# Block 2's mixer: v and u before q and k, q and k with stationary weights, and three quarters of wo's pooled half ahead of the last heads' value products

## The chip, the cores and the metric

The kernel runs on one core of a Trainium2 chip. The metric is the device time of one execution in microseconds (us); lower is better. A core has a matrix engine (TensorE, PE in the profile; its weight loads are PEld), a vector engine (DVE), an activation engine (ACT), a small general engine (POOL), and a queue engine that issues DMAs (SP). Each engine works through its own list of instructions in the order in which the program holds them.

## The reference, cut to what matters

The program computes three transformer layers for 256 tokens of width 1024: twice a "first block", then one "second block" (block 2). The change lies in the mixer of block 2. In float32:

```python
h = rmsnorm(x, g_mix_pre) * (1 + scale_m) + shift_m       # 256 x 1024
q, k, v, u = split(h @ w_in)                              # each 256 x 512
z = q . k / sqrt(64)              # 8 heads of 64, keys before the query only
log1m = -softplus(z)              # masked
after = reverse_cumsum(log1m) - log1m
w = exp(log_sigmoid(z) + after)   # masked: stick-breaking weights
attn = w @ v                                              # 256 x 512
pool = ((trailing means of u over 2, 4, 8, 16 tokens) - u) @ w_pool * pool_scale
mix = concat(attn, pool) @ w_out                          # 256 x 1024
x = x + gate_m * rmsnorm(mix, g_mix_post)
```

A feed-forward part follows it and ends the program.

## The kernel before, in words

**Weights.** All weights come from one packed array in the order that `stream_order` lists. Each entry of the list is a chunk of two halves of 512 KB. SP loads a half into a `raw` tile (7 buffers). ACT then rounds it into a tile `H` (line 278) and DVE makes the remainder `L` = raw - H (line 280), 12 buffers each. A product of float32 exactness is made of three products of the rounded kind: H times the high part of the activations, H times their low part, and L times the high part. The activations are held in `Pair` tiles: `xm` for the normalised input of the mixer, `m` for its output (`m20` to `m23`: `m20` and `m21` hold the attention half, `m22` and `m23` the pooled half).

**Two forms of product.** `mmA4` keeps the activations stationary: for one of the two token tiles (t = 0 or 1, 128 tokens each), 24 matmuls of 512 columns give 128 tokens x 512 outputs. `mmB` keeps the weights stationary: for 128 outputs, 8 matmuls of 512 columns (both tiles' high and low parts side by side) and 8 of 256 columns give 128 outputs x 256 tokens, which is the transposed result. `mmD2` is a step of wo: two contraction chunks, one tile t, one half c of the output columns, 6 matmuls of 512 columns.

**Order on TensorE.** The program text is recorded in one order, and small pieces of work are put between the large products by a clock kept by hand: `pe(ns)` advances it, a generator that yields d is resumed by `tick()` once d us of this clock have passed. A scheduler then settles the order on each engine; `tc.high_priority` pulls instructions ahead, `issue_after` pins an order.

**The mixer of block 2.** `mixer2` makes q and k with `mmA4`, tile by tile; `turn` copies each result out (ACT, line 1005), lets TensorE transpose it (4 transposes into `pt2q` or `pt2k`, line 1009), and DVE copies it into `qT` or `kT` (line 1012). Then come v and u (`pv`, `pu`). Between these products stand the heads: `stick` handles four heads at a time, heads (0,1) of the pairs 0 and 1 as `z00` to `z11`, those of the pairs 2 and 3 as `z20` to `z31`. For each it makes the scores `z<-qT,kT`, then on DVE the mask and on ACT Abs, Exp and Ln and on DVE a sum (together softplus, into a tile `e1`), then on TensorE the running sums `z<-e1,tri`, on ACT an Exp, and then for the four heads together the value products `po2<-e1,v2`, whose result ACT and DVE put into `m` (lines 211, 212). `pool` makes, for each of the four groups g, `pl` (two matmuls with `pmat`), copies it out on ACT (`pm`, line 1040), multiplies by `w_pool` (`ppl`) and writes `m22` or `m23` on ACT and DVE (lines 1046, 1047).

**After the mixer.** The main text issues, on ACT's queue, five loads of gains and of modulation rows (`gpm`, `mpm`, `ggf`, `mgf`, `sh_f`), two of which DVE multiplies (`gpm`, `ggf`). Then the steps of wo follow. `WO2_LEAD` says how many of the four pairs (tile t, pooled chunk i) are recorded before the last heads are drained; the rest follows, with the norm of each tile (`Post`, `Norm`), and the feed-forward part begins with `pgA`.

Of the kernel before, what the change touches and what calls it, by code (L numbers as in the profile page):

```python
# [12 lines left out]
AF = mybir.ActivationFunctionType  # L13
ALU = mybir.AluOpType
# [30 lines left out]
TR_GAP = 0.0  # L45
LEAD = 1
MIX_DELAY = 2.5
WO2_LEAD = 2
UNIT = 10.0
SM_DELAY = 8.0  # L50
SOFT = 30
ST_DELAY = 8.0
ST_STEP = 3.5


# [38 lines left out]
def stream_order():  # L94
    o = []
    cond = list(COND)
    for l in range(DEPTH):
        o += [("q", l, c, h) for c in range(2) for h in range(2)]
        o += [("kv", l, h) for h in range(2)]
        for j in range(4):  # L100
            o += [("cc", l, j), ("cx", l, j), ("cb", l, j)]
        for n in ("cp", "gb", "ga", "ap"):
            o += four(n, l, take_cond(cond, n, l))
        o += [("wo", l, j) for j in range(4)]
        o += ffn_order(l, take_cond(cond, "ffn", l))
    assert not cond
    o += [("q2", h) for h in range(2)]
    o += [("k2", h) for h in range(2)]
    o += [("v2", h) for h in range(2)]
    o += [("u2", h) for h in range(2)]  # L110
    o += [("wo", 2, j) for j in (2, 3, 0, 1)]
    o += ffn_order(2, [])
    return o
# [5 lines left out]
def pack_weights(inp):  # L119
    splits = dict(q=0, kv=1024, cb=1536, cc=2560, cx=3584, ga=4608, gb=5632)  # L120
    out = np.empty((len(ORDER), P, CH), np.float32)

    def put(i, w, r0, nk, c0, nc_):
        src = w[r0:r0 + nk * P, c0:c0 + nc_]
        if nk == 4:
            out[i].reshape(P, nk, nc_)[...] = src.reshape(nk, P, nc_).transpose(1, 0, 2)
        else:
            out[i].reshape(P, 2, nk, nc_ // 2)[...] = src.reshape(nk, P, 2, nc_ // 2).transpose(1, 2, 0, 3)

    for i, k in enumerate(ORDER):  # L130
        n = k[0]
        if n == "q":
            put(i, inp["w_in"][k[1]], 512 * k[3], 4, 512 * k[2], 512)
        elif n == "kv":
            put(i, inp["w_in"][k[1]], 512 * k[2], 4, 1024, 512)
        elif n in ("cc", "cx", "cb"):
            put(i, inp["w_in"][k[1]], 0, 8, splits[n] + 256 * k[2], 256)
        elif n in ("ga", "gb", "cp", "ap"):
            w = {"cp": "w_conv_proj", "ap": "w_attn_proj"}.get(n, "w_in")
            put(i, inp[w][k[1]], 512 * (k[2] % 2), 4, splits.get(n, 0) + 512 * (k[2] // 2), 512)  # L140
        elif n == "cond":
            w = inp["w_cond_2"][0][:, 1024 * k[1]:1024 * (k[1] + 1)].reshape(D, P, KT)
            out[i].reshape(P, 2, D)[...] = w[:, :, 2 * k[2]:2 * k[2] + 2].transpose(1, 2, 0)
        elif n in ("q2", "k2", "v2", "u2"):
            put(i, inp["w_in_2"][0], 512 * k[1], 4, 512 * ("q2", "k2", "v2", "u2").index(n), 512)
        else:
            l = k[1]
            sfx, li = ("", l) if l < 2 else ("_2", 0)
            if n == "wo":
                put(i, inp["w_out" + sfx][li], 256 * k[2], 2, 0, 1024)  # L150
            elif n == "d":
                put(i, inp["w_down" + sfx][li], 256 * k[2], 2, 0, 1024)
            elif n in ("gA", "uA"):
                w = inp[("w_gate" if n == "gA" else "w_up") + sfx][li]
                put(i, w, 512 * k[2], 4, 0, 512)
            else:
                w = inp[("w_gate" if n == "g" else "w_up") + sfx][li]
                put(i, w, 0, 8, 512 + 256 * k[2], 256)
    return out
# [3 lines left out]
def tile_model(ctx: ExitStack, tc: tile.TileContext, x_in, wpack, sink, convw, gains, c_in,  # L163
# [55 lines left out]
    def spawn(gen, delay=0.0):  # L219
        tasks.append([clock[0] + delay, gen])  # L220

    def pe(ns):
        clock[0] += ns / 1000.0
# [20 lines left out]
            pass  # L244

    def mm(o, a, b, start, stop, **kw):
        nc.tensor.matmul(o, a, b, start=start, stop=stop, **kw)  # L247


    state = dict(raw=0, spl=0, use=0, behind=None, a=None, v=None)  # L250
# [699 lines left out]
    def stick(hps, qT, kT, v2, mp):  # L950

        rs = [slice(e * HD, (e + 1) * HD) for e in range(2)]
        hes = [(hp, e) for hp in hps for e in range(2)]
        z = {he: ps1(f"z{he[0]}{he[1]}") for he in hes}
        for hp in hps:
            for e in range(2):
                mm(z[hp, e][:, 0:T], kT[rs[e], hp, 0:P], qT[rs[e], hp, :], True, False, skip_group_check=True)
            for e in range(2):
                mm(z[hp, e][:, T:T + P], kT[rs[e], hp, P:T], qT[rs[e], hp, P:T], False, False, skip_group_check=True)
            pe(650)  # L960
        sps = {}
        for he in hes:
            zz = z[he][:, 0:384]
            z3 = zz.rearrange("p (b t) -> p b t", b=3)
            nc.vector.tensor_add(z3[:, 0:3:2, :], z3[:, 0:3:2, :], smask.unsqueeze(1).to_broadcast([P, 2, P]))
            e1 = s2(f"e1_{he[0]}{he[1]}", (P, 384))
            nc.scalar.activation(e1, zz, AF.Abs)
            nc.scalar.activation(e1, e1, AF.Exp, scale=-1.0)
            nc.scalar.activation(e1, e1, AF.Ln, bias=1.0)
            nc.vector.scalar_tensor_tensor(e1, zz, 0.0, e1, ALU.max, ALU.add)  # L970
# [21 lines left out]
    def mixer2(xp, norms):  # L992
        mp = Pair("m2")
        qT = s4("qT2", (P, 4, T))
        kT = s4("kT2", (P, 4, T))
# [1 line left out]
        u2t = s4("u2", (P, 2, 512))  # L997
        v2 = [v2t[:, t, :] for t in range(2)]
        cap = 2 * state["use"] + 8
        ww = {n: [get((n, h), cap) for h in range(2)] for n in ("q2", "k2")}  # L1000

        def turn(nm, t, ps, dstT, scl):
            tk = s2(f"tk2{nm}{t}")
            with ahead():
                state["behind"] = (nc.scalar.activation(tk, ps, AF.Copy, scale=scl), state["behind"][1])
            yield 1.5
            pt = ps1(f"pt2{nm}{t}", (P, 4, P))
            for k in range(4):
                nc.tensor.transpose(pt[:, k, :], tk[:, k * P:(k + 1) * P], ident)
                pe(107)  # L1010
            with ahead():
                nc.vector.tensor_copy(dstT[:, :, t * P:(t + 1) * P], pt)
            yield None

        for t in range(2):
            finish(norms[t].gen)
            for nm, dstT, scl in (("q2", qT, 0.125), ("k2", kT, 1.0)):
                ps = ps1(f"p2{nm}{t}")
                mmA4(ps, ww[nm], xp, t)
                spawn(turn(nm, t, ps, dstT, scl))  # L1020
                tick()
                if t == 0 and nm == "k2":
                    wv = [get(("v2", h), cap + 4) for h in range(2)]
        for i in range(2):
            spawn(stick((2 * i, 2 * i + 1), qT, kT, v2, mp), 3.0 + 4 * ST_STEP * i)
        for n, dst in (("v2", v2t), ("u2", u2t)):
            w = wv if n == "v2" else [get((n, h), cap + 8) for h in range(2)]
            for t in range(2):
# [24 lines left out]
        for g in range(4):  # L1053
            if g < 3:
                next(gens[g + 1])
            next(gens[g])
        return mp


# [166 lines left out]
```

## Time and profile before

| | |
|---|---|
| median of 3 runs | 1144.59 us (1143.29 to 1145.06) |
| the profiled execution | 1144.54 us, of which its span from first to last instruction is 1142.4 us |
| TensorE matmuls busy | 1132.2 us, 99% of the span |
| TensorE weight loads busy | 951.7 us, 83% |
| DVE busy | 800.3 us, 70% |
| ACT busy | 687.2 us, 60% |
| mean granted clock of TensorE | 0.998 of full speed |

The 2.1 us between the span and the time of the execution lie outside the recorded instructions. Busy times of TensorE are modelled from the starts of pipelined matmuls, so the distance from one start to the next is the better measure of what a matmul costs, and the rows below are read in that way.

### The profile page before, as it was taken

What the parts mean: (1) busy time and instruction counts of PE and PEld (TensorE: products, weight loads), DVE (VectorE), ACT (ScalarE), POOL (GpSimd) and SP (SyncE); (2) the same over time, 40 slices, a digit from 0 to 9 for tenths busy, and PEclk for the clock granted to TensorE, in tenths of its full rate; (3) what the DMA queues carried; (4) which work ended last, traced back from release to release, by engine and by line L of the source; (5) the groups of instructions that cost most, each with busy time, mean ns of one, the idle gap of its engine ahead of it and who ended that gap; (6) DMA issues with size and microseconds to landing.
All of it is one profiled execution on the core that took longest, in us unless ns stands there. A gap on an engine that the chain in (4) does not pass through costs nothing.

```text
span 1142.4 us, 15967 instructions
## 1 busy us (share of the span) xinstructions
PE 1132.2 (99%) x5901; PEld 951.7 (83%) x5901; DVE 800.3 (70%) x1188; ACT 687.2 (60%) x1209; POOL 13.4 (1%) x28
## 2 busy tenths in 40 slices
PE   8999999999999999999999999999999999999997
PEld 5888878888888888888878888888888778888886
DVE  7888745658977657798874758977657748866652
ACT  6778766547555446688765556545445847655441
POOL 0000000000000000000000000000000000000000
PEclk9999999999999999999999999999999999999999
DMA  7944346537987752835686538987773653855610
GB/s 286 367 131 160 118 148 210 187 137 253 351 286 244 248 203 85 303 129 166 203 269 211 178 118 275 354 275 243 254 265 104 228 167 110 312 185 185 200 58 37
DMA packets 67039, 235.39 MB, mean 206 GB/s; under 512 B 8849, under 2 KB 9361, under 8 KB 66962
## 3 DMA queue, kind: packets, MB, share of 16 engines
q1 hardware_dynamic: 63216, 224.83, 57.3%
q10 hardware_dynamic: 3746, 9.56, 2.5%
q8 instruction: 46, 0.75, 0.3%
q14 instruction: 31, 0.25, 0.1%
HBM read 233.28 MB, written 1.07 MB: 205 GB/s over the span
## 4 chain that ended last, share of the span: by engine, by line
PE 95%; DMA 2%; DVE 1%; issue 1%; ACT 0%; DVEq 0%; POOLq 0%; POOL 0%; ACTq 0%; SPq 0%
PE dn L247 15%; PE pu L247 14%; PE pg L247 13%; PE wo L247 5%; PE pcc L247 4%; PE pap L247 4%; PE pgb L247 4%; PE pga L247 4%; PE pcx L247 4%; PE pcp L247 4%; PE pcb L247 3%; PE pq L247 3%; PE puA L247 3%; PE pgA L247 3%; PE pkv L247 2%; PE po L247 1%
## 5 line engine op out<-in xcount | busy, mean ns | idle before, releaser
L280 DVE TENSOR_TENSOR L<-raw,H 128x1024 fp32r<-128x1024 f32 x370 | 445.4, 1220 | 141.1 <-ACT H L278 131.5
L278 ACT CAST H<-raw 128x1024 fp32r<-128x1024 f32 x370 | 383.5, 1052 | 153.8 <-issue 40.8
L247 PE MATMUL dn<-H,fHL 128*128 128x512 f32 x432 | 116.1, 390 | 0.0
L247 PE MATMUL pu<-xf,H 128*128 128x512 f32 x432 | 108.2, 392 | 0.0
L247 PE MATMUL pg<-xf,H 128*128 128x512 f32 x432 | 107.8, 391 | 0.0
L247 PEld LDWEIGHTS dn<-H,fHL 128*128 128x128 f32 x432 | 79.8, 188 | 15.6
L247 PEld LDWEIGHTS pg<-xf,H 128*128 128x128 f32 x432 | 79.2, 188 | 15.2
L247 PEld LDWEIGHTS pu<-xf,H 128*128 128x128 f32 x432 | 77.7, 189 | 13.9
L528 DVE SCALAR_TENSOR_TENSOR raw<-raw,silu_c 128x1024 f32<-128x1024 f32 x48 | 58.4, 1219 | 27.0 <-DMA raw<-in_wpack_dram 26.9
L247 PE MATMUL dn<-L,fHL 128*128 128x512 f32 x216 | 66.6, 389 | 0.0
L247 PEld LDWEIGHTS pg<-xf,L 128*128 128x128 f32 x432 | 58.9, 190 | 4.2
L247 PEld LDWEIGHTS pu<-xf,L 128*128 128x128 f32 x432 | 58.9, 190 | 4.2
L247 PE MATMUL pu<-xf,L 128*128 128x256 f32 x432 | 60.2, 282 | 0.0
L247 PE MATMUL pg<-xf,L 128*128 128x256 f32 x432 | 60.2, 282 | 0.0
L247 PE MATMUL wo<-H,m 128*128 128x512 f32 x192 | 52.9, 396 | 0.1
L575 ACT CAST fHL<-f 128x512 fp32r<-128x512 f32 x27 | 16.7, 620 | 54.1 <-DVE f L573 54.1
L247 PEld LDWEIGHTS dn<-L,fHL 128*128 128x128 f32 x216 | 40.5, 188 | 8.6
L569 ACT ACTIVATE s<-s 128x512 f32<-128x512 f32 x27 | 17.1, 632 | 43.4 <-DVE s L458 43.3
L247 PEld LDWEIGHTS wo<-H,m 128*128 128x128 f32 x192 | 35.4, 188 | 8.1 <-DVE m L212 0.6
L247 PE MATMUL pap<-H,o 128*128 128x512 f32 x128 | 35.2, 394 | 0.0
L247 PE MATMUL pcp<-H,y 128*128 128x512 f32 x128 | 35.1, 395 | 0.0
L670 ACT ACTIVATE P<-S,nm 128x256 f32<-128x256 f32 x64 | 29.5, 478 | 3.5 <-DVE nm L664 3.5
(290 smaller groups left out, 1927.6 us busy)
## 6 DMA issues: line engine op xcount, KB each, us to landing
raw<-in_wpack_dram SPq DMA_DIRECT2D x422, 512.0 KB, 5.1
gpm<-in_gains_dram ACTq DMA_DIRECT2D x3, 512.0 KB, 7.9
gpf<-in_gains_dram ACTq DMA_DIRECT2D x3, 512.0 KB, 8.9
gqf<-in_gains_dram ACTq DMA_DIRECT2D x2, 512.0 KB, 6.5
out_dram<-x SPq DMA_DIRECT2D x4, 256.0 KB, 2.0
pmat<-in_pmat_dram SPq DMA_DIRECT2D x2, 384.0 KB, 7.4
x<-in_x_dram SPq DMA_DIRECT2D x2, 256.0 KB, 3.0
x<-in_x_dram SPq DMA_DIRECT2D x1, 512.0 KB, 7.0
```

Source lines behind the costliest of these rows:

```text
L247: nc.tensor.matmul(o, a, b, start=start, stop=stop, **kw)
L278: nc.scalar.copy(H, r)
L280: nc.vector.tensor_sub(L, r, H.bitcast(F32))
L528: nc.vector.scalar_tensor_tensor(w[u], w[u], 1.0, silu_c, ALU.mult, ALU.mult, accum_out=mcol[:, r, 2 * j + u:2 * j + u + 1])
L569: last = nc.scalar.activation(s, s, AF.Silu)
L575: nc.scalar.copy(fHL[:, 0], fv)
L670: nc.scalar.activation(Pt[:, hh, :], S[hh // 2][:, hh % 2, :], AF.Exp, bias=nm[:, hh:hh + 1], accum_out=den[:, hh:hh + 1])
```

## The change

The chunks of v and u come first in the packed array, then q and k by halves of their output (256 outputs, or two pairs of heads, each): q half 0, k half 0, q half 1, k half 1. v and u are made with `mmA4`, tile by tile. q and k are made with `mmB`, so that their results come out transposed; `both2` writes them into `qT` and `kT` (an ACT copy with a scale and a DVE sum for each 128 outputs), and `turn` with its transposes is gone. `sticks` starts the first four heads once half 0 is there, and the second four after k's half 1. The delays of `stick` differ, its vector and activation work gets a raised priority, and the running sums are pinned behind the matmul recorded before them. `WO2_LEAD` is 3 instead of 2. The core of the diff:

```diff
-WO2_LEAD = 2
+WO2_LEAD = 3
-ST_DELAY = 8.0
+ST_DELAY = 5.5
@@ stream_order
-    o += [("q2", h) for h in range(2)]
-    o += [("k2", h) for h in range(2)]
     o += [("v2", h) for h in range(2)]
     o += [("u2", h) for h in range(2)]
+    for h in range(2):
+        o += [("q2", h), ("k2", h)]
@@ stick
+        yield 0.0
         sps = {}
         for he in hes:
...
+            with tc.high_priority(offset=SOFT):
+                nc.vector.tensor_add(z3[:, 0:3:2, :], z3[:, 0:3:2, :], smask.unsqueeze(1).to_broadcast([P, 2, P]))
+                e1 = s2(f"e1_{he[0]}{he[1]}", (P, 384))
+                nc.scalar.activation(e1, zz, AF.Abs)
+                nc.scalar.activation(e1, e1, AF.Exp, scale=-1.0)
+                nc.scalar.activation(e1, e1, AF.Ln, bias=1.0)
+                nc.vector.scalar_tensor_tensor(e1, zz, 0.0, e1, ALU.max, ALU.add)
             sps[he] = e1
-        yield ST_DELAY
+        yield ST_DELAY + (2.0 if hps[0] else 0.0)
         for n, he in enumerate(hes):
-            mm(z[he][:, 0:384], tri[:, 0, :], sps[he], False, False, skip_group_check=True)
+            with tc.issue_after(state["pe"].ins):
+                mm(z[he][:, 0:384], tri[:, 0, :], sps[he], False, False, skip_group_check=True)
             mm(z[he][:, P:T], tri[:, 1, :], sps[he][:, T:T + P], False, True, skip_group_check=True)
             pe(870)
-            nc.scalar.activation(sps[he], z[he][:, 0:384], AF.Exp)
+            with tc.high_priority(offset=SOFT):
+                nc.scalar.activation(sps[he], z[he][:, 0:384], AF.Exp)
             if n == 1:
-                yield 2.0
+                yield 0.0 if hps[0] else 2.5
@@ new
+    def sticks(ready, qT, kT, v2, mp):
+        first, second = (stick(hps, qT, kT, v2, mp) for hps in ((0, 1), (2, 3)))
+        for _ in range(3):
+            yield next(first)
+        next(first)
+        while not ready():
+            yield 0.5
+        yield 0.3
+        next(second)
+        yield 0.5
+        next(first)
+        for d in second:
+            yield d
@@ mixer2
-        ww = {n: [get((n, h), cap) for h in range(2)] for n in ("q2", "k2")}
-        def turn(nm, t, ps, dstT, scl):
...
+        ww = {n: [get((n, h), cap) for h in range(2)] for n in ("v2", "u2")}
         for t in range(2):
             finish(norms[t].gen)
-            for nm, dstT, scl in (("q2", qT, 0.125), ("k2", kT, 1.0)):
-                ps = ps1(f"p2{nm}{t}")
-                mmA4(ps, ww[nm], xp, t)
-                spawn(turn(nm, t, ps, dstT, scl))
...
-        for i in range(2):
-            spawn(stick((2 * i, 2 * i + 1), qT, kT, v2, mp), 3.0 + 4 * ST_STEP * i)
...
+            for n, dst in (("v2", v2t), ("u2", u2t)):
                 ps = ps1(f"p{n}{t}")
-                mmA4(ps, w, xp, t)
+                mmA4(ps, ww[n], xp, t)
                 nc.scalar.copy(dst[:, t, :], ps)
+        def both2(dst, o, scl):
+            nc.scalar.activation(dst, o[:, 1], AF.Copy, scale=scl)
+            nc.vector.scalar_tensor_tensor(dst, o[:, 0], scl, dst, ALU.mult, ALU.add)
+        for h in range(2):
+            for nm, dst, scl in (("q2", qT, 0.125), ("k2", kT, 1.0)):
+                mmB(f"p{nm}{h}", get((nm, h)), xp, lambda c, o: both2(dst[:, 2 * h + c, :], o, scl))
+            if h == 0:
+                spawn(sticks(lambda: state["k2"], qT, kT, v2, mp), 1.0)
+        state["k2"] = True
```

The order on the engines at three places. In the names, the digits behind the last underscore number the tile. First, TensorE in the middle of q, before: a tile of q (`p2q21`) with the transposes of k in between.

```order
L247 MATMUL p2q21_8522<-H166_0_8199,xm20_8337 128x512 x4
L247 MATMUL p2q21_8522<-L166_0_8200,xm20_8337 128x512 x2
L247 MATMUL p2q21_8522<-H166_1_8203,xm21_8340 128x512 x4
L247 MATMUL p2q21_8522<-L166_1_8204,xm21_8340 128x512 x2
L1009 MATMUL pt2k20_8535<-ident_78,tk2k20_8496 128x128 x4
L247 MATMUL p2q21_8522<-H167_0_8207,xm22_8354 128x512 x4
L247 MATMUL p2q21_8522<-L167_0_8208,xm22_8354 128x512 x2
```

The same engine at the start of q in the changed kernel, directly behind the last of u:

```order
L249 MATMUL pq20_0_8570<-xm20_8337,H170_0_8546 128x512 x2
L249 MATMUL pq20_0_8570<-xm21_8340,H170_0_8546 128x512 x2
L249 MATMUL pq20_0_8570<-xm22_8354,H170_0_8546 128x512 x2
L249 MATMUL pq20_0_8570<-xm23_8357,H170_0_8546 128x512 x2
L249 MATMUL pq20_0_8570<-xm20_8337,L170_0_8547 128x256 x2
L249 MATMUL pq20_0_8570<-xm21_8340,L170_0_8547 128x256 x2
L249 MATMUL pq20_0_8570<-xm22_8354,L170_0_8547 128x256 x2
L249 MATMUL pq20_0_8570<-xm23_8357,L170_0_8547 128x256 x2
```

Of 24 matmuls of 512 columns for each tile and four transposes, there are now 16 matmuls for each 128 outputs, half of them of 256 columns, and no transposes. Second, TensorE at the end of the pooled part, before:

```order
L247 MATMUL ppl0_8834<-pm0_8827,wpool_8386 128x256
L247 MATMUL pl2_8839<-pmat1_8383,u2_8395 128x256
L247 MATMUL pl2_8839<-pmat1_8383,u2_8395 128x128
L247 MATMUL ppl1_8844<-pm1_8832,wpool_8386 128x256
L247 MATMUL pl3_8848<-pmat1_8383,u2_8395 128x256
L247 MATMUL pl3_8848<-pmat1_8383,u2_8395 128x128
L247 MATMUL ppl2_8853<-pm2_8842,wpool_8386 128x256
L247 MATMUL z31_8734<-e1_31_8762,tri_8384 128x128
L247 MATMUL ppl3_8858<-pm3_8851,wpool_8386 128x256
L247 MATMUL wo2_00_8874<-H174_0_8882,m22_8836 128x512 x4
```

and in the changed kernel, behind the scores of the second four heads, `pl2` and the first four of the eight value products `po20`:

```order
L249 MATMUL po20_8838<-e1_10_8714,v2_8394 64x256
L249 MATMUL po20_8838<-e1_11_8720,v2_8394 64x256
L249 MATMUL po20_8838<-e1_10_8714,v2_8394 64x128
L249 MATMUL po20_8838<-e1_11_8720,v2_8394 64x128
L249 MATMUL ppl1_8874<-pm1_8808,wpool_8386 128x256
L249 MATMUL pl3_8878<-pmat1_8383,u2_8395 128x256
L249 MATMUL pl3_8878<-pmat1_8383,u2_8395 128x128
L249 MATMUL ppl2_8883<-pm2_8836,wpool_8386 128x256
L249 MATMUL ppl3_8888<-pm3_8881,wpool_8386 128x256
L249 MATMUL wo2_00_8904<-H174_0_8662,m22_8818 128x512 x4
L249 MATMUL wo2_00_8904<-L174_0_8663,m22_8818 128x512 x2
```

The running sums of the last heads no longer stand among the pooled products: `ppl2`, `ppl3` and wo's first step follow each other directly. Third, ACT at the same place, before:

```order
L1040 COPY pm0_8827<-pl0_8824 128x256
L1040 COPY pm1_8832<-pl1_8829 128x256
L977 ACTIVATE e1_30_8756<-z30_8733 128x384
L1046 ACTIVATE m22_8836<-ppl0_8834,pscale_127 128x256
L1040 COPY pm2_8842<-pl2_8839 128x256
L1046 ACTIVATE m22_8836<-ppl1_8844,pscale_127 128x256
L1040 COPY pm3_8851<-pl3_8848 128x256
L1046 ACTIVATE m23_8855<-ppl2_8853,pscale_127 128x256
```

and in the changed kernel, where `pm2`'s copy and three Abs of the second four heads (line 971) stand just ahead of the first row:

```order
L971 ACTIVATE e1_31_8869<-z31_8824 128x384
L972 ACTIVATE e1_21_8857<-e1_21_8857 128x384
L972 ACTIVATE e1_20_8851<-e1_20_8851 128x384
L972 ACTIVATE e1_30_8863<-e1_30_8863 128x384
L972 ACTIVATE e1_31_8869<-e1_31_8869 128x384
L973 ACTIVATE e1_20_8851<-e1_20_8851 128x384
L973 ACTIVATE e1_30_8863<-e1_30_8863 128x384
L973 ACTIVATE e1_31_8869<-e1_31_8869 128x384
L973 ACTIVATE e1_21_8857<-e1_21_8857 128x384
L213 CAST m20_8847<-po20_8838 128x2x256
L1054 ACTIVATE m22_8818<-ppl1_8874,pscale_127 128x256
L1048 COPY pm3_8881<-pl3_8878 128x256
```

Between the copies `pm2` and `pm3` there now stand fourteen activations instead of one.

## Rows read from the trace of the kernel before

**Rows 1.** The page, part 1: busy time of each engine, its share of the span, instructions.

```profile
PE 1132.2 (99%) x5901; PEld 951.7 (83%) x5901; DVE 800.3 (70%) x1188; ACT 687.2 (60%) x1209; POOL 13.4 (1%) x28
```

**Rows 2.** First the table by stretches, for the stretch from the first product of q to the first of `pgA`: the stretch, its length, busy time (and instructions) of PE, PEld, DVE, ACT and POOL, the granted clock, the DMA share and GB/s. Then, from the list of TensorE's waits over the whole span, the longest one outside the first 20 us: total, times, longest.

```profile
862.80:951.60 88.80, 88.65 (x443) 70.46 (x442) 55.46 (x77) 53.93 (x106) 2.23 (x4) 1.00 0.48 160
PE pq L644 <- DVE qs L639: 0.9, 1, 0.9
```

**Rows 3.** Timeline of TensorE in q (start, length, line, operation, tiles, shape, count): two half chunks of six matmuls with the four transposes of k between them.

```profile
876.54 1.07 PE L247 MATMUL p2q<-H,xm 128*128 128x512 f32 x4
...
877.91 0.60 PE L1009 MATMUL pt2k<-ident,tk2k 128*128 128x128 f32 x4
...
879.74 1.07 PE L247 MATMUL p2q<-H,xm 128*128 128x512 f32 x4
```

**Rows 4.** The same timeline in layer 1's feed-forward part, where `mmB` runs four times (`pg` twice, `pu` twice): the first matmuls of the first, and the matmuls that follow the fourth.

```profile
812.45 1.98 PE L247 MATMUL pg<-xf,H 128*128 128x512 f32 x8
...
823.60 1.09 PE L247 MATMUL dn<-H,fHL 128*128 128x512 f32 x4
```

**Rows 5.** The same timeline at the small products between the large ones: scores (`z<-qT,kT`), running sums (`z<-e,tri`, whose row at 909.07 is left out), value products (`po`), pooled products (`pl`, `ppl`), each with the large products behind it.

```profile
891.10 0.63 PE L247 MATMUL pv<-L,xm 128*128 128x512 f32 x2
891.66 1.58 PE L247 MATMUL z<-qT,kT 64*128 64x256 f32 x16
893.17 1.20 PE L247 MATMUL pv<-H,xm 128*128 128x512 f32 x4
...
894.67 1.08 PE L247 MATMUL pv<-H,xm 128*128 128x512 f32 x4
...
910.72 1.18 PE L247 MATMUL pu<-H,xm 128*128 128x512 f32 x4
...
912.20 1.09 PE L247 MATMUL pu<-H,xm 128*128 128x512 f32 x4
...
913.67 1.52 PE L247 MATMUL po<-e,v 128*64 128x256 f32 x16
915.12 1.20 PE L247 MATMUL pu<-H,xm 128*128 128x512 f32 x4
...
916.61 1.90 PE L247 MATMUL z<-e,tri 128*128 128x384 f32 x8
...
922.56 0.59 PE L247 MATMUL ppl<-pm,wpool 128*128 128x256 f32 x2
922.99 0.82 PE L247 MATMUL pl<-pmat,u 128*128 128x256 f32 x4
923.64 0.60 PE L247 MATMUL ppl<-pm,wpool 128*128 128x256 f32 x2
...
925.76 1.28 PE L247 MATMUL wo<-H,m 128*128 128x512 f32 x4
...
927.33 1.09 PE L247 MATMUL wo<-H,m 128*128 128x512 f32 x4
```

**Rows 6.** The same timeline in wo: the last value products in two parts, and a row of seven matmuls of wo.

```profile
930.16 1.30 PE L247 MATMUL po<-e,v 128*64 128x256 f32 x10
931.39 1.19 PE L247 MATMUL wo<-H,m 128*128 128x512 f32 x4
...
935.03 0.86 PE L247 MATMUL po<-e,v 128*64 128x256 f32 x6
935.82 0.50 PE L247 MATMUL wo<-H,m 128*128 128x512 f32 x1
...
936.64 2.20 PE L247 MATMUL wo<-H,m 128*128 128x512 f32 x7
```

**Rows 7.** Timeline of ACT: the first and the last row of the run of twelve activations (Abs, Exp, Ln of the first four heads) is given by the start of its first two and of what follows the twelfth; then the copy of the value products into `m`, two copies `pm` in a row, and a scaled copy of a pooled product into `m`.

```profile
895.27 0.87 ACT L967 ACTIVATE e<-z 128x384 f32<-128x384 f32 x2
...
900.08 0.59 ACT L1031 COPY v<-pv 128x512 f32<-128x512 f32 x1
...
915.52 0.57 ACT L211 CAST m<-po 128x512 fp32r<-128x512 f32 x1
...
921.66 0.65 ACT L1040 COPY pm<-pl 128x256 f32<-128x256 f32 x2 [0.66 <-PE pl L247]
...
923.19 0.47 ACT L1046 ACTIVATE m<-ppl,pscale 128x256 fp32r<-128x256 f32 x1 [0.48 <-PE ppl L247]
```

**Rows 8.** TensorE's clock at both ends of the program. First the table by stretches for the first matmuls (length, PE busy and matmuls, granted clock, DMA share, GB/s; the clock is not recorded this early and shown as 1.00), then the durations of the matmuls that open the program (ns, least, median, most), then the table by stretches, with all engines, behind the last matmul.

```profile
1.40:5.60 4.20, 4.15 (x10) 1.00 0.77 253
L247 PE MATMUL warm_ps<-warm x17: 379/607/634, 1.5 to 9.0; 128*128 128x512 bf16 x17
1136.20:1138.80 2.60, 0.00 (x0) 0.00 (x0) 1.57 (x3) 0.98 (x3) 0.55 (x1) 1.00 0.00 0
1138.90:1142.40 3.50, 0.00 (x0) 0.00 (x0) 0.44 (x1) 0.00 (x0) 0.00 (x0) 0.50 0.40 150
```

**Rows 9.** The load of the modulation row `mgf` (engine, size, us from issue to landing), and DVE's timeline: the product that waits for it and the low part of the last heads behind that.

```profile
mgf<-modd ACTq DMA_DIRECT2D x1, 512.0 KB, 8.9
936.00 1.23 DVE L1124 SCALAR_TENSOR_TENSOR ggf<-mgf,ggf 128x1024 f32<-128x1024 f32 x1 [1.47 <-DMA mgf<-modd]
937.14 0.68 DVE L212 TENSOR_TENSOR m<-po,m 128x512 fp32r<-128x512 f32 x1
```

**Rows 10.** Groups by line from 862 to 952 us, shapes apart: DVE's remainders `L` of the weights, busy time, mean ns of one, idle time before them and what ended it.

```profile
L280 DVE TENSOR_TENSOR L<-raw,H 128x1024 fp32r<-128x1024 f32 x22 | 26.0, 1218 | 7.7 <-ACT H L278 7.7
```

More of the change, by code (lines that the diff above doesn't have):

```diff
@@ L143, in pack_weights @@
             out[i].reshape(P, 2, D)[...] = w[:, :, 2 * k[2]:2 * k[2] + 2].transpose(1, 2, 0)
-        elif n in ("q2", "k2", "v2", "u2"):
-            put(i, inp["w_in_2"][0], 512 * k[1], 4, 512 * ("q2", "k2", "v2", "u2").index(n), 512)
+        elif n in ("q2", "k2"):
+            put(i, inp["w_in_2"][0], 0, 8, 512 * ("q2", "k2").index(n) + 256 * k[1], 256)
+        elif n in ("v2", "u2"):
+            put(i, inp["w_in_2"][0], 512 * k[1], 4, 1024 + 512 * ("v2", "u2").index(n), 512)
         else:
@@ L246, in mm @@
     def mm(o, a, b, start, stop, **kw):
-        nc.tensor.matmul(o, a, b, start=start, stop=stop, **kw)
+        state["pe"] = nc.tensor.matmul(o, a, b, start=start, stop=stop, **kw)
     state = dict(raw=0, spl=0, use=0, behind=None, a=None, v=None)
@@ L964, in stick @@
             z3 = zz.rearrange("p (b t) -> p b t", b=3)
[L965 to L970, printed above, removed]
+            with tc.high_priority(offset=SOFT):
[5 more added lines that the diff above has]
+                nc.vector.scalar_tensor_tensor(e1, zz, 0.0, e1, ALU.max, ALU.add)
             sps[he] = e1
-        yield ST_DELAY
+        yield ST_DELAY + (2.0 if hps[0] else 0.0)
         for n, he in enumerate(hes):
-            mm(z[he][:, 0:384], tri[:, 0, :], sps[he], False, False, skip_group_check=True)
+            with tc.issue_after(state["pe"].ins):
+                mm(z[he][:, 0:384], tri[:, 0, :], sps[he], False, False, skip_group_check=True)
             mm(z[he][:, P:T], tri[:, 1, :], sps[he][:, T:T + P], False, True, skip_group_check=True)
             pe(870)
-            nc.scalar.activation(sps[he], z[he][:, 0:384], AF.Exp)
+            with tc.high_priority(offset=SOFT):
+                nc.scalar.activation(sps[he], z[he][:, 0:384], AF.Exp)
             if n == 1:
-                yield 2.0
+                yield 0.0 if hps[0] else 2.5
         yield 2.0
@@ L990, in stick @@
         yield None
+    def sticks(ready, qT, kT, v2, mp):
[11 more added lines that the diff above has]
+            yield d
     def mixer2(xp, norms):
+        state["k2"] = False
         mp = Pair("m2")
@@ L999, in mixer2 @@
         cap = 2 * state["use"] + 8
-        ww = {n: [get((n, h), cap) for h in range(2)] for n in ("q2", "k2")}
-        def turn(nm, t, ps, dstT, scl):
[L1003 to L1013, printed above, removed]
+        ww = {n: [get((n, h), cap) for h in range(2)] for n in ("v2", "u2")}
         for t in range(2):
             finish(norms[t].gen)
-            for nm, dstT, scl in (("q2", qT, 0.125), ("k2", kT, 1.0)):
-                ps = ps1(f"p2{nm}{t}")
-                mmA4(ps, ww[nm], xp, t)
-                spawn(turn(nm, t, ps, dstT, scl))
-                tick()
-                if t == 0 and nm == "k2":
-                    wv = [get(("v2", h), cap + 4) for h in range(2)]
-        for i in range(2):
-            spawn(stick((2 * i, 2 * i + 1), qT, kT, v2, mp), 3.0 + 4 * ST_STEP * i)
-        for n, dst in (("v2", v2t), ("u2", u2t)):
-            w = wv if n == "v2" else [get((n, h), cap + 8) for h in range(2)]
-            for t in range(2):
+            for n, dst in (("v2", v2t), ("u2", u2t)):
                 ps = ps1(f"p{n}{t}")
-                mmA4(ps, w, xp, t)
+                mmA4(ps, ww[n], xp, t)
                 nc.scalar.copy(dst[:, t, :], ps)
+        def both2(dst, o, scl):
[7 more added lines that the diff above has]
+        state["k2"] = True
         def pool(g):
@@ L1055, in mixer2 @@
                 next(gens[g + 1])
+            tick()
             next(gens[g])
+            tick()
         return mp
```

## The prediction, made before the changed kernel was run

> **What bounds the kernel now.** I read the page's busy times first [rows 1]: TensorE is busy 99% of the span and has more work than any other engine. Then the stage: from the first product of q to the first of `pgA` 88.80 us pass, TensorE is busy 88.65 of them, at full clock, and the longest wait anywhere outside the first 20 us is 0.9 us, in another stage [rows 2]. So nothing ends last here but TensorE's own stream. DVE and ACT are busy about 55 us of the 88.80; a faster copy or softplus buys nothing. The change can act in two ways only: by shortening TensorE's list, or by putting a wait into it. I therefore read the starts of its rows (the distance from one start to the next is the price), and then look on the engines that serve it for anything that is late.
>
> The profiled execution took 1144.54 us, the median is 1144.59, so the sum below is made against 1144.54 and needs no correction. A measurement of this kernel can tell about 0.2%, 2.3 us, from no change.
>
> **Transposes removed.** Half a chunk of q is six matmuls. With the four transposes behind it, it takes 879.74 - 876.54 = 3.20 us for two halves, and the first half alone 877.91 - 876.54 = 1.37 [rows 3]. Four transposes thus cost 3.20 - 2.73 = 0.47. There are four such groups: **-1.9 us**.
>
> **q and k in the other form.** Before: 4 tiles of 4 halves of six matmuls at 1.36 each, 4 x 4 x 1.36 = 21.8. After: 8 runs of `mmB`. Four of them took 823.60 - 812.45 = 11.15 us in layer 1, 2.79 each [rows 4]; 8 x 2.79 = 22.3. **+0.5 us**: half of the matmuls now have 256 columns, which cost a little over half of one of 512. The Trainium skill ("TensorE: Matmul & The Clock Gate", section "Back-to-back issue gap") gives a smaller gap for each matmul; as an estimate by that page the two forms would differ by some 0.1 us, and the sum would be 0.4 lower. The rows include what the loads between matmuls cost, so they decide here.
>
> **Small products among the large ones.** A large product behind a group of small ones starts late, and differently so by kind. A large matmul follows another after 1.36 / 6 = 0.227 us. The first four large ones behind the scores are booked 1.20 long instead of 1.08 or 1.09, behind the running sums 1.18, behind the value products 1.20, behind the pooled products 1.28 [rows 5]. With about 0.1 at the entry where two row-tiled products are involved, an island costs 0.25 (scores), 0.12 (sums), 0.23 (values), 0.21 (pooled). Before there are two islands of scores, three of sums that stand alone, one of values and the pooled block: 0.50 + 0.36 + 0.23 + 0.21. The last value products come in two parts, 931.39 - 930.16 = 1.23 and 935.82 - 935.03 = 0.79, together 2.02 against 1.45 in one piece (913.67 to 915.12); with two exits and entries instead of none I count 0.99 for it. Right behind, seven wo matmuls are booked 2.20, where six at 0.227 and a last one of 0.39 (1.07 for four, less three [rows 3]) make 1.75: 0.45 lost in a short wait [rows 6]. Sum before 2.74. After: the first scores alone (0.25), two islands of sums (0.24), one block of scores, `pl2`, values and pooled products (0.24, between 0 and 0.48), its end (0.21), the last sums and values in one island (0.23): 1.2. **-1.6 us**, from -1.3 to -1.8. Nearly all that three quarters of wo's pooled half buys lies in here, the split and the 0.45: TensorE hardly waited for the last heads before, so a larger reserve of work ahead of them has little more to cover.
>
> So far -1.9 + 0.5 - 1.6 = -3.0 us.
>
> **A new wait: `ppl3` for `pm3`.** TensorE now has, behind `pl2`, the value products of the first heads, `ppl1`, `pl3`, `ppl2`, `ppl3`, and then wo, with nothing large in between. `ppl3` needs the copy `pm3`, and on ACT this stands behind the copy of `pm2`, the twelve activations of the second four heads, the cast of `m20` and the scaling of `m22`. ACT may start this row only when `pl2`'s result is there: a `pl` is booked 0.82 and the next matmul starts after 0.65, so 0.17 later [rows 5]. Then come the two copies (0.65 together), twelve activations (900.08 - 895.27 = 4.81), the cast (0.57) and the scaling (0.47) [rows 7]: 0.17 + 6.50 = 6.7, less about 0.2 because neighbours overlap a little: 6.5 us. TensorE fills 1.45 (values), 0.43 (`ppl1`), 0.65 (`pl3`), 0.43 (`ppl2`) [rows 5], with two entries of 0.1 some 3.2 us. **Stall +3.3 us**. Its bounds: 3.0, if all fourteen overlap as much as the closest rows; 4.0, if an Abs waits besides for DVE's mask. Everything behind it is held up, since TensorE takes its list in order: the wo steps on `m22`, though ready, can't pass `ppl3`. Before, only one scaling stood between the two copies, and `pm3` was never late.
>
> **The clock.** After the last matmul of the program the granted clock is still 1.00 until 1138.80, 2.6 us after 1136.20, and 0.50 from 1138.90 on [rows 8]. So idleness of about 2.7 us was enough there for the lower level, and the stall is longer. What the lower level costs shows at the program's start: ten matmuls of 512 columns took 4.20 us, 0.42 each, against 0.227 later, before the rate rose: 4.20 - 2.27 = 1.9 us lost [rows 8]. Bounds: 0 (the clock holds) and 2.0. I take **+1.6 us**, near the one row that shows a rise from idle, a little below since the first product behind the stall is a small one. The Trainium skill ("TensorE: Matmul & The Clock Gate", section "HAM oscillation — how this bites in real kernels") speaks against the change in just this way: waits on other engines let the clock drop to its lower level, and the work behind each begins at 1.2 GHz. The end of this trace agrees that idleness lowers it; that a wait in mid-program does so, no row here shows, for there is none that long.
>
> **Costed at nothing.** The 16 halves of q, k, v and u come in another order, but each is still rounded once; in the 22.3 us of q and k DVE makes 8 remainders of 1.22 [rows 10], 9.8 us, with 8 sums of `both2` beside them, half of its time. If one were late, each would show as a gap ahead of a large product. The scores of a pair follow `both2` of k with at least one `mmB` of 2.79 us between for the first heads; the second heads' scores have the pooled products `ppl0` and one more `pl` ahead, some 2.6 us against some 1.9 for the last copy and sum. The first heads' softplus lies under k's second half. The last low part of `m21` stands on DVE behind `ggf`, which waited 1.47 us for `mgf`, 8.9 us after its issue [rows 9]; the five loads now stand on ACT's queue behind the pooled scalings, which I count to leave some 2 us.
>
> **The rivals.**
>
> *The stall is there, the clock holds.* For it: 2.7 and 3.3 us are near each other, and the first falls behind a long stretch of large matmuls while the second falls behind small ones; against: the row is the only measure there is, and it is passed. Time: 1144.54 - 3.0 + 3.3 = 1144.9.
>
> *The stall isn't there, or is short.* This needs ACT's row at 3.2 us or so instead of 6.5, with activations of some 0.15 us each, which no row shows. Only a much later arrival of TensorE at `ppl3`, by a wait ahead of `pl2` that lets ACT run on, could shrink it, and that moves the loss only. Time: 1144.54 - 3.0 = 1141.6, up to 1142.2 with a rest. This is the side on which the change gains.
>
> *Slower than before.* The low part of `m21` comes late, on top of the likeliest case: `mpm` and `mgf`, for which DVE waits ahead of it, are issued on ACT behind the scaled copies, and so later by the same stall. If `mgf` lands more than about 11 us after its issue (8.9 before [rows 9]), DVE stands at `ggf` (1.23 us) while the wo steps that don't need `m21` run out, and the last ones wait, 1 to 2 us. Against it: 2 us of margin at the landing time seen. Time: 1146.5 + 1.6 = 1148.1, a change of +0.3%.
>
> **How the numbers follow.** Likeliest, the stall with a lowered clock: -3.0 + 3.3 + 1.6 = +1.9, 1146.5 us, chance 0.45, its own range 1145.3 to 1147.8. The stall with a steady clock 0.33, 1144.9. No stall 0.09, 1141.6. The late `m21` 0.13, 1148.1. The lines for measurable differences are 1142.3 and 1146.9: the first case is split by the second line, about 0.2 of its 0.45 beyond it; with the last case slower has 0.33. Faster is the third case, 0.09; 0.58 remain for no measurable difference. Range: 1142.8 to 1148.6, which leaves out the third case and the far end of the last.
>
> **What would show it.** Right: no `pt2q` or `pt2k`; 2.79 us for each 128 outputs of q and k; in TensorE's waits one of about 3.3 us of `ppl3` on ACT's copy at line 1048, with ACT busy through it with lines 971 to 973; behind it a stretch at granted clock 0.5, some 3.5 us long; the stage about 90.7 us. Wrong: `ppl3` waits under 1 us (the ACT row is mis-sized, or stands elsewhere); the clock stays at 1.00 behind it (the fifth term is 0); gaps ahead of `pq` or `pk` (a late weight); or a wait ahead of the last wo steps on `m21` or on the last Exp.

## The result, and the profile after

The changed kernel takes 1146.77 us (median of 20 runs, 1143.98 to 1149.39); the kernel before takes 1144.20 beside it (20 runs). The ratio is 1.0023, with a 95% interval from 1.0017 to 1.0029: a little slower, at the line of what can be told from no change. The forecast was 1146.5, a change of +1.9 us; the medians differ by 2.6, the profiled executions by 1.8 (1146.31 against 1144.54). The span of the profiled execution is 1144.3 us. A few executions of the experiments were disturbed (1404.12, 2921.79 and 6469.61 us) and are left out of what follows.

The page, part 1, of the changed kernel, as in [rows 1]:

```profile
PE 1131.3 (99%) x5917; PEld 953.4 (83%) x5917; DVE 799.9 (70%) x1192; ACT 687.1 (60%) x1213; POOL 13.5 (1%) x28
```

These shares say nothing of what happened; TensorE was even busy 0.9 us less. The table by stretches does (columns as in [rows 2]). First the whole stage, now from the first product of v to the first of `pgA`, then four stretches in it:

```profile
862.59:953.67 91.08, 87.71 (x459) 71.68 (x458) 54.70 (x79) 54.16 (x109) 2.24 (x4) 0.98 0.45 156
...
919.74:923.70 3.96, 0.60 (x4) 0.20 (x2) 2.35 (x5) 3.96 (x11) 0.00 (x0) 1.00 0.39 125
923.70:925.40 1.70, 1.69 (x5) 1.35 (x6) 1.12 (x4) 0.82 (x2) 0.00 (x0) 0.58 0.06 22
925.40:927.10 1.70, 1.70 (x6) 1.33 (x5) 0.34 (x1) 0.00 (x0) 0.00 (x0) 0.50 0.67 224
927.10:928.60 1.50, 1.50 (x7) 1.24 (x6) 0.00 (x0) 0.00 (x0) 0.00 (x0) 0.90 1.05 311
```

The stage takes 91.08 us instead of 88.80, which is 2.28 more; the rest of the program takes 0.4 less, and its code is the same. TensorE is idle for 3.4 us in the second row, in which ACT is busy from end to end. Behind that the clock is at its lower level for some 3.4 us and full again from 927.4 or so. TensorE's waits hold one new line:

```profile
PE ppl L249 <- ACT pm L1048: 3.4, 1, 3.4
```

TensorE's timeline, first two of the eight products of q and k and what follows the first pair, then around the wait:

```profile
885.41 1.98 PE L249 MATMUL pq<-xm,H 128*128 128x512 f32 x8
...
888.17 2.00 PE L249 MATMUL pq<-xm,H 128*128 128x512 f32 x8
...
890.97 2.00 PE L249 MATMUL pk<-xm,H 128*128 128x512 f32 x8
...
917.11 1.52 PE L249 MATMUL po<-e,v 128*64 128x256 f32 x16
...
919.74 0.60 PE L249 MATMUL ppl<-pm,wpool 128*128 128x256 f32 x2
923.71 0.99 PE L249 MATMUL ppl<-pm,wpool 128*128 128x256 f32 x2 [3.37 <-ACT pm L1048]
924.15 2.27 PE L249 MATMUL wo<-H,m 128*128 128x512 f32 x4
926.21 1.06 PE L249 MATMUL wo<-L,m 128*128 128x512 f32 x2
...
928.61 1.08 PE L249 MATMUL wo<-H,m 128*128 128x512 f32 x4
```

And ACT's in the same time:

```profile
917.21 0.37 ACT L1048 COPY pm<-pl 128x256 f32<-128x256 f32 x1 [1.88 <-PE pl L249]
917.48 1.78 ACT L971 ACTIVATE e<-z 128x384 f32<-128x384 f32 x4
919.13 1.77 ACT L972 ACTIVATE e<-e 128x384 f32<-128x384 f32 x4
...
921.20 1.35 ACT L973 ACTIVATE e<-e 128x384 f32<-128x384 f32 x3
922.44 0.59 ACT L213 CAST m<-po 128x512 fp32r<-128x512 f32 x1
922.90 0.50 ACT L1054 ACTIVATE m<-ppl,pscale 128x256 fp32r<-128x256 f32 x1
923.27 0.39 ACT L1048 COPY pm<-pl 128x256 f32<-128x256 f32 x1
```

From `pm2`'s copy to `pm3`'s, ACT works without a gap: twelve activations, the cast of `m20`, the scaling of `m22`. `pm3` is there at 923.66, and `ppl3` starts at 923.71. The large matmuls behind it start 0.4 to 0.5 us apart instead of 0.23 until about 927.

### The profile page after: what moved, and what is told of

Its sections match the earlier page's. It is cut to its first block, busy times and chain, and to the rows that moved or that the text cites. A ratio compares the mean times of both kernels' runs of the same rounds, so it can differ in the third digit from the quotient of the medians.

```text
span 1144.3 us, 16022 instructions
## 1 busy us (share of the span) xinstructions
PE 1131.3 (99%) x5917; PEld 953.4 (83%) x5917; DVE 799.9 (70%) x1192; ACT 687.1 (60%) x1213; POOL 13.5 (1%) x28
```

## The experiments

Each kernel is the changed one with the edit shown, unless said otherwise. "Stage" is the distance from the first large product of the mixer to the first of `pgA` in the profiled execution, 88.81 us before (951.64 - 862.83, by the starts of these two products) and 91.08 in the changed kernel.

### The copy ahead of softplus

```diff
-            if g < 3:
+            if g < 2:
                 next(gens[g + 1])
+            if g == 1:
+                next(gens[3])
```

> The changed kernel with one difference: the last pooled product pl3 is recorded directly behind pl2, so its copy pm3 stands on ACT ahead of the twelve softplus activations of the second four heads instead of behind them. Theory (the wait of ppl3 for pm3, 3.37 us, and the low clock behind it, 1.6 us, are the whole loss; the rest of the change shortened TensorE's list by 2.7 us): no wait of ppl3, clock 1.00 throughout the stage, 5.0 us less than the changed kernel, 2.7 us less than before. Rival one (the wait only moves: softplus ends later by a copy, and the running sums of the last heads wait for it instead): a wait of 1 us or more at the sums, gain under 3 us on the changed kernel. Rival two (the shorter list is not real and the loss lies elsewhere): about the time of before.

Measured: 1147.50 us against 1143.82 (ratio 1.0034, 1.0022 to 1.0047); the stage takes 91.70. The wait of `ppl3` is gone, and a longer one has come. The list of waits, the first product of wo on TensorE's timeline, DVE's row that ends just ahead of it, and the table by stretches:

```profile
PE wo L249 <- DVE m L214: 4.3, 1, 4.3
```

```profile
925.73 2.05 PE L249 MATMUL wo<-H,m 128*128 128x512 f32 x4 [4.30 <-DVE m L214]
```

```profile
924.90 0.68 DVE L214 TENSOR_TENSOR m<-po,m 128x512 fp32r<-128x512 f32 x1
```

```profile
921.40:925.70 4.30, 0.03 (x1) 0.00 (x0) 2.66 (x6) 4.30 (x11) 0.00 (x0) 0.94 0.41 125
925.70:926.70 1.00, 0.97 (x2) 0.83 (x3) 1.00 (x3) 0.12 (x1) 0.00 (x0) 0.50 0.99 406
```

The wait did move, but not to the running sums, as the rival had it. wo's first step reads `m22`, and yet it is released by the low part of `m20` (line 214), which it doesn't read. What joins the two is the PSUM bank, the piece of TensorE's result memory that a product fills: in the compiled program `po20`, from which `m20` is made, and `wo2_00` lie in the same bank, and the first matmul of `wo2_00` waits for the instruction that makes the low part of `m20`. `m20`'s cast stands on ACT behind the twelve activations. So there are several things behind softplus on ACT (the copy `pm3`, the cast that frees `po20`'s bank, three of the four scalings that wo's steps read), and freeing one of them uncovers the next. The theory of one late copy falls; that the copy is what ended the wait in the changed kernel stays.

### Useless work in the gap, in `ppl3`'s own bank

```diff
             ps = ps1(f"ppl{g}")
+            if g == 3:
+                for _ in range(7):
+                    mm(ps[:, 0:T], u2t[:, 0, gs], pmat[0][:, 0, 0:T], True, True)
             mm(ps[:, 0:T], wpool[:, g, :], pm, True, True)
```

> The changed kernel with seven useless fp32 matmuls of 256 columns (0.43 us each, 3.0 us) into the bank of ppl3, ahead of ppl3, whose own product then starts the bank anew. ACT's order and the time at which pm3 is ready stay as they are. Theory (the idleness itself lowers the clock): ppl3 starts at the same place, the wait left is about 0.4 us, the clock stays at 1.00 behind it, and the time falls by the clock's share alone, 1.6 us, to about 1.0 us above before. Rival one (the clock falls for another reason, as the small products or ACT's load): the stretch at 0.50 stays, and the time is that of the changed kernel. Rival two (the useless work delays ppl3): slower than the changed kernel by up to 3 us.

> The same with three useless matmuls, 1.3 us of work, which leaves 2.1 us of idleness ahead of ppl3. At the program's end the clock held through 2.6 us of idleness. Theory (a wait shorter than about 2.7 us leaves the clock alone): no low stretch, the same time as with seven, 1.0 us above before. Rival (any wait of some us costs clock): a low stretch behind ppl3, and a time near the changed kernel, 2.3 us above before.

Measured: with seven 1149.89 us (ratio 1.0052, 1.0040 to 1.0065), with three 1148.40 (1.0042, 1.0030 to 1.0055). Both miss what they were made for: `ppl3` lies in the bank of `pl3`, which `pm3`'s copy frees, so the useless matmuls wait as long as `ppl3` did and come on top. TensorE's timeline and four stretches of the kernel with seven:

```profile
924.08 6.13 PE L249 MATMUL ppl<-pmat,u 128*128 128x256 f32 x14 [3.37 <-ACT pm L1048]
930.05 0.59 PE L249 MATMUL ppl<-pm,wpool 128*128 128x256 f32 x2
```

```profile
920.70:924.00 3.30, 0.01 (x1) 0.00 (x0) 2.29 (x5) 3.30 (x10) 0.00 (x0) 0.85 0.40 117
924.00:925.00 1.00, 0.92 (x2) 0.83 (x3) 1.00 (x3) 0.40 (x2) 0.00 (x0) 0.50 0.92 340
...
929.50:930.00 0.50, 0.50 (x3) 0.41 (x2) 0.00 (x0) 0.00 (x0) 0.00 (x0) 0.64 0.00 0
930.00:931.00 1.00, 1.00 (x6) 0.84 (x6) 0.00 (x0) 0.32 (x1) 0.00 (x0) 1.00 0.00 0
```

They took 5.97 us (924.08 to 930.05) instead of 3.0, since the clock was low until about 929.9. It had fallen within the wait, at about 923.0, so the low level lasted 6.8 us here and 3.4 in the changed kernel, behind the same wait of 3.37 us. That need not be the kernel's doing: this execution (1150.95 us) is the only one of five with a mean clock of 0.995; the other four have 0.998 and took 1148.80 to 1150.52.

With three useless matmuls the trace shows the same wait, and full clock through all of it:

```profile
923.55 2.29 PE L249 MATMUL ppl<-pmat,u 128*128 128x256 f32 x6 [3.37 <-ACT pm L1048]
```

```profile
923.00:924.00 1.00, 0.45 (x2) 0.42 (x3) 1.00 (x3) 0.88 (x3) 0.00 (x0) 1.00 0.90 262
924.00:925.00 1.00, 1.00 (x5) 0.81 (x4) 0.52 (x2) 0.00 (x0) 0.00 (x0) 0.62 0.98 401
...
927.00:928.00 1.00, 1.00 (x5) 0.81 (x4) 0.76 (x2) 0.21 (x1) 0.00 (x0) 0.67 0.21 74
```

The clock fell at about 924.2, when TensorE had been at work again for 0.7 us, and was full again at 927.7. So neither kernel tests what it was made for, whether the clock falls without the wait.

### The same work one product earlier, where the bank is free

The edit is the same with `g == 2`: the useless matmuls go into the bank of `ppl2`, ahead of `ppl2`.

> The changed kernel with seven useless fp32 matmuls of 256 columns (3.0 us) ahead of ppl2, in ppl2's bank, which is free at that time. ACT's order stays; pm3 is ready when it was. Theory (idleness lowers the clock): a wait of some 0.35 us is left ahead of ppl3, the clock stays at 1.00 behind it, the stage ends 1.6 us earlier than that of the changed kernel, about 1 us above before. Rival (the clock falls for another reason, as long runs of the small fp32 products): a stretch at 0.50 as before, and the time of the changed kernel or more.

> The same with three useless matmuls, 1.3 us, which leave 2.1 us of idleness ahead of ppl3. Theory (idleness has to last some 2.7 us, as at the program's end): clock 1.00 behind it, the same time as with seven. Rival (it does not need to last that long where small products stand around it): a low stretch, 1 to 2 us more than with seven.

Measured: with seven 1144.77 us against 1144.27 (ratio 1.0008, 0.9999 to 1.0017), stage 89.47; with three 1145.99 (1.0017, 1.0008 to 1.0027), stage 89.44. Of the kernel with seven, TensorE's rows from the useless work on, and the clock behind the wait:

```profile
918.83 3.19 PE L249 MATMUL ppl<-pmat,u 128*128 128x256 f32 x14
...
922.80 0.70 PE L249 MATMUL ppl<-pm,wpool 128*128 128x256 f32 x2 [0.35 <-ACT pm L1048]
923.15 1.28 PE L249 MATMUL wo<-H,m 128*128 128x512 f32 x4
...
926.10 1.07 PE L249 MATMUL wo<-H,m 128*128 128x512 f32 x4
```

```profile
923.50:924.50 1.00, 1.00 (x6) 0.78 (x6) 0.72 (x2) 0.47 (x1) 0.00 (x0) 1.00 0.91 344
```

and of the kernel with three:

```profile
920.19 1.46 PE L249 MATMUL ppl<-pmat,u 128*128 128x256 f32 x6
...
924.15 0.70 PE L249 MATMUL ppl<-pm,wpool 128*128 128x256 f32 x2 [2.07 <-ACT pm L1048]
```

```profile
924.50:925.50 1.00, 1.00 (x6) 0.84 (x5) 0.72 (x3) 0.47 (x1) 0.00 (x0) 1.00 0.18 74
```

Here ACT is as late as ever, and TensorE is kept at work for 3.0 or 1.3 us of the time it would stand idle. In both traces the clock stays full, with 0.35 us of idleness left and with 2.07. From the start of `ppl3` over the same thirteen products to the next, it takes 926.10 - 922.80 = 3.30 us, where the changed kernel takes 928.61 - 923.71 = 4.90: the clock's share is 1.60 us, and the stage is shorter by that much (91.08 - 89.47 = 1.61). So the idleness is what cost the clock, and ACT's lateness without it cost none. The kernel with seven bears this out beyond its trace: its median is 2.0 us under that of the changed kernel (the kernel before took 1144.27 and 1144.20 beside the two), with mean clocks of 0.998 to 1.000 against 0.995 to 0.999.

For the kernel with three only the traced execution shows it, the fastest one (1145.00 us, mean clock 0.999). The nine others took 1145.77 to 1146.78 at 0.998, and the median lies 1.2 us above that of the kernel with seven, as far as the rival forecast. The two traced executions differ by as much, and there the difference lies ahead of the stage, which starts at 861.68 with seven and at 863.04 with three, in code that is the same, while the stages agree to 0.03. Whether the clock fell in some of the nine others is open.

### The whole pooled part ahead of the second four heads

```diff
-        state["k2"] = True
-
         def pool(g):
...
             next(gens[g])
             tick()
+        state["k2"] = True
+        for _ in range(4):
+            tick(clock[0] + 1.0)
         return mp
```

> The changed kernel with the second four heads started behind the whole pooled part: TensorE makes pl2, ppl1, pl3, ppl2, ppl3, then the scores of the second four heads and the first heads' value products, then the three pairs of wo steps. On ACT all four pooled scalings then stand ahead of the twelve activations, and wo's 8.2 us lie over these. Theory (what had to be cleared from behind softplus was the whole way of the pooled half into m22 and m23, not the copy pm3 alone; once it is, only the shorter list of TensorE is left): no wait above 0.5 us in the stage, clock 1.00 throughout it, 2.3 to 2.8 us less than before, about 5 us less than the changed kernel. Rival (the ACT work of the last heads can't be covered in this order: the wait moves on to the running sums, which need softplus): a wait of 1 us or more at the sums or the last value products, and a time between before and the changed kernel.

> The kernel with the pooled part first, with two pairs of wo steps ahead of the last heads instead of three. Theory (the third pair covers nothing: from the end of the last scores value products and two pairs give 6.9 us, the twelve activations with the mask and the sum take about 6.2): within 1.0 us of the same kernel with three pairs, slightly above for the islands in the split steps. Rival (the third pair is what hides softplus): a wait of 1.5 us or more at the sums, and more than 1.5 us above.

Measured: 1141.46 us against 1144.27 (ratio 0.9977, 0.9969 to 0.9986), and with two pairs ahead 1141.99 (0.9982, 0.9973 to 0.9991). Of the kernel with three pairs, the stage, then ACT (last pooled scaling, first activations, the cast of `m20`), then TensorE:

```profile
862.67:948.63 85.96, 85.88 (x460) 70.43 (x458) 54.82 (x79) 54.36 (x109) 2.24 (x4) 1.00 0.47 166
```

```profile
917.89 0.47 ACT L1052 ACTIVATE m<-ppl,pscale 128x256 fp32r<-128x256 f32 x1 [0.31 <-PE ppl L249]
919.31 0.87 ACT L971 ACTIVATE e<-z 128x384 f32<-128x384 f32 x2 [0.95 <-DVE z L969]
...
924.12 0.60 ACT L213 CAST m<-po 128x512 fp32r<-128x512 f32 x1
```

```profile
919.29 1.52 PE L249 MATMUL po<-e,v 128*64 128x256 f32 x16
920.74 1.20 PE L249 MATMUL wo<-H,m 128*128 128x512 f32 x4
...
929.04 3.63 PE L249 MATMUL z<-e,tri 128*128 128x384 f32 x16
```

The high parts of the pooled half are written by 918.4, and softplus (919.31 to 924.1) lies under the value products and wo. The stage is 85.96 us, TensorE is busy 85.88 of it at full clock. The last softplus, with DVE's sum, is ready at 925.0, some 4 us before the running sums at 929.04, so the third pair has nothing to cover; without it the time is 0.5 us more, inside both intervals. This version beats both kernels by their medians, by 2.8 us and by 5.3.

The kernel with `pl3` early was also run with two pairs:

> The first of these kernels (pm3 early) with two pairs of wo steps instead of three ahead of the last heads. Theory (the third pair covers nothing, since softplus of the last heads ends before two pairs have run, 5.4 us): the sums of the last heads don't wait for softplus; only their last Exp, 0.5 us, lies bare between sums and value products, so 0.3 to 0.7 us above the first kernel. Rival (the reserve is needed): a wait of 2 us or more at the sums, 2 us or more above the first kernel.

Measured: 1147.77 us (ratio 1.0037, 1.0023 to 1.0050), 0.3 above the one with three, with the same 4.3 us wait of wo on line 214. Since that wait was not foreseen, it tells only that the third pair made no difference behind it.

### Three pairs of wo alone

The kernel before with one number changed.

```diff
-WO2_LEAD = 2
+WO2_LEAD = 3
```

> The kernel before with three pairs of wo steps ahead of the last heads instead of two, and nothing else. Theory (TensorE hardly waited for the last heads, so the third pair only joins the split value products, 0.54 us, and removes the short wait of 0.45 behind them): no wait to be seen in the stage, the value products in one piece of 1.45 us, the stage 0.5 to 1.2 us shorter than before. Rival one (the third pair is the useful part of the change): 2 us or more shorter. Rival two (it only shifts the order): the same within 0.3 us.

Measured: 1143.82 us against 1144.31 (ratio 0.9995, 0.9987 to 1.0004); the stage takes 950.71 - 862.34 = 88.37, 0.44 less. TensorE's rows of the last value products:

```profile
929.76 1.29 PE L247 MATMUL po<-e,v 128*64 128x256 f32 x10
...
934.62 0.86 PE L247 MATMUL po<-e,v 128*64 128x256 f32 x6
```

They still come in two parts, ten and six, as in [rows 6], so the theory missed that half. The row of wo that lost 0.45 before is gone, and that is all that the third pair brings to the stage; the whole times can't be told apart.

### q and k first, in the new form

```diff
-    o += [("v2", h) for h in range(2)]
-    o += [("u2", h) for h in range(2)]
     for h in range(2):
         o += [("q2", h), ("k2", h)]
+    o += [("v2", h) for h in range(2)]
+    o += [("u2", h) for h in range(2)]
```

The products are in the same order, and `state["k2"]` is set once v is made.

> The changed kernel with q and k ahead of v and u, as before the change, but in the new form with stationary weights; the second four heads start once v is made. Theory (in this form the first product of q needs the normalised input of both token tiles, and that of tile 1 comes late: in the changed kernel its transposes stand 8.3 and 10.1 us behind the start of the stage): TensorE waits ahead of the first or second product of q, 3 to 8 us, with a low clock behind it, and the time is 2 to 8 us above before; behind that, no wait at the pooled part, since all softplus lies under v and u. Rival (tile 1 is ready when it is wanted, and only stands late in the program's order): no wait, and 2.5 us less than before, as with the pooled part first.

Measured: 1150.25 us against 1144.31 (ratio 1.0060, 1.0046 to 1.0073). The waits, and the table by stretches behind the first of them:

```profile
PE pt_nm L407 <- DVE xg_nm L397: 5.7, 1, 5.7
...
PE pl L249 <- ACT u L1039: 0.3, 1, 0.3
```

```profile
868.64:870.70 2.06, 1.99 (x9) 1.59 (x9) 0.94 (x2) 0.45 (x2) 0.00 (x0) 0.50 0.00 0
```

TensorE stands 5.7 us for the normalised input of tile 1, which v and u of tile 0 hide in the changed kernel, and the clock falls as well. At the pooled part no wait is left but one of 0.3. So in the new form q and k can't stand first without such a wait, at least in this version; with v and u first, the second heads' softplus comes next to the pooled part, and there the loss arose.

## Why the prediction was right, step by step

**The wait.** Forecast 3.3 us of `ppl3` for `pm3`; measured 3.37. From the start of the value products behind `pl2` (917.11) to the end of `pm3` (923.66) 6.55 us pass, and the sum of rows was 6.5. What it did not hold is that the same ACT row has more standing behind it than `pm3`: the prediction said that wo's steps on `m22` were ready and held up by `ppl3` alone. That is wrong. The second scaling of `m22` was made at 922.90, behind softplus as well, and `wo2_00` had no bank before `m20` was out of `po20`. For the time of this kernel it made no difference, since both were done before `ppl3` was (924.15): the scaling at 923.40, the low part of `m20`, the later of the two things that free its bank, at 923.90 by DVE's row:

```profile
923.22 0.68 DVE L214 TENSOR_TENSOR m<-po,m 128x512 fp32r<-128x512 f32 x1
```

For the remedy it decided, as the kernel with `pl3` early shows.

**The clock.** Forecast 1.6 us; measured 1.60. The mechanism is shown by the seven useless matmuls ahead of `ppl2`: same lateness, hardly any idleness, full clock. The Trainium skill ("TensorE: Matmul & The Clock Gate", section "HAM oscillation — how this bites in real kernels") was taken to speak against the change: it tells of waits for DMAs, behind which the clock is at its lower level and the next matmuls start slow. The rows here agree for a wait on ACT, at 0.50 of full clock from 924.0 to 927.4. That the size came out to a tenth is partly luck: it was taken from a row of the program's start, and behind the same wait of 3.37 us the low stretch lasted 3.4 us in two traces and 6.8 in a third.

**The shorter list.** Forecast -3.0 us; the stage gives 2.28 - 3.37 - 1.60 = -2.7. The transposes are gone. One product of 128 outputs takes 2.76 to 2.80 us (888.17 - 885.41, 890.97 - 888.17), forecast 2.79, so eight of them against 21.8 us are +0.5 as forecast; with the forecast's own -1.9 for the transposes, which no run takes apart, the two make -1.4. For the islands -1.3 is then left, at the edge of the forecast's -1.3 to -1.8: this term was too large by 0.3. The kernel with the pooled part first, in which nothing waits, agrees with the whole: 85.96 - 88.81 = -2.85. The forecast's reading of wo's lead was half wrong. The third pair alone took 0.44 us from the stage, the wait in the row of seven; the value products stayed split, and stand in one piece only with the other edits.

**What was costed at nothing.** No product of q or k waited for a weight, the first heads' scores and sums waited for nothing, and the last low part of `m21` was in time. These covers held.

**The rivals.** "The stall is there, the clock holds" is what the kernels with useless work ahead of `ppl2` show: stages of 89.47 and 89.44, some 0.65 above before, where the forecast's rival had 0.3. In one of the changed kernel's 20 executions the mean clock was 0.999 and the time 1143.98, where most had 0.997 or 0.998 and 1145.2 to 1147.3, and six had 0.995 and 1147.2 to 1149.4. That the clock held in the one and was low for longer in the six is likely, but not shown; only one execution has a trace, at 0.998. The traced execution at 0.995 of the kernel with seven useless matmuls in `ppl3`'s bank speaks for it, with its low stretch of 6.8 us. "No stall" is the kernel with the pooled part first: 1141.46, where the rival had 1141.6. The late `m21` didn't come.

## What to carry to other kernels

When a piece of work is pulled ahead on one engine, list everything that then stands behind it on the engine that serves it, copies and casts that free a bank as much as results, and ask for each who waits; moving one item out uncovers the next. Here the gain of 2.8 us was real, and a burst of twelve activations placed ahead of four short ones turned it into a loss of 2.3; starting that burst behind the short ones brought it back. Count the clock with the wait: here 3.37 us of idleness cost 1.60 more behind it.

## What the runs showed of the hardware

The length of the idleness alone doesn't tell when the clock falls. From the mean clock of the stretches, it fell this long behind the end of TensorE's last product: 3.6 us in the changed kernel (0.58 over 923.70 to 925.40, so at 924.0, against 920.3), 3.8 with `pl3` early (0.94 over 921.40 to 925.70, so at 925.2, against 921.4), 2.3 with seven useless products in `ppl3`'s bank (0.85 over 920.70 to 924.00, so at 923.0, against 920.7), 4.0 with three of them (0.62 over 924.00 to 925.00, so at 924.2, against 920.2), and 2.7 at the program's end [rows 8]. In the changed kernel and in that with three, TensorE was already at work again when it fell, for 0.3 and 0.7 us. In the one trace with a wait of 2.07 us it didn't fall.

The lower level didn't last equally long either: 3.4 us in the changed kernel (to 927.4), with `pl3` early (to 928.6) and with three useless products (to 927.7), and 6.8 us with seven (to 929.9). What decides between these, no run settles.
